# Per-column softmax scaling on ScalarE, split GpSimd subtractions, one more scratch buffer, and a new order of the first loads

## The chip, the core and the metric

The kernel runs on one core of one Trainium2 chip. A core has TensorE (PE, matrix multiplication, with its weight loads shown apart as PEld), VectorE (DVE), ScalarE (ACT), GpSimd (POOL) and SyncE (SP, which here only issues transfers). Each engine takes its own instructions in order; they wait for each other through semaphores. The metric is the device time of one execution in microseconds (us).

## The reference

One decoder layer on x of 512 tokens by 1024 channels. One projection of x gives the inputs of three mixers that run side by side, and the gates:

```python
u = jnp.einsum('bsd,de->bse', x, w_in) + b_in
y_a = _pool_mixer(a_x, pool_w, pool_b, pool_scale) * silu(a_z)      # trailing means, windows 2, 4, 8, 16
y_b = _dsa_mixer(b_q, b_k, b_v, i_q, i_k, i_w) * silu(b_z)          # attention over the top keys of an indexer
y_c = _nsa_mixer(c_q, ..., c_g, ...) * silu(c_z)                    # compressed, selected and window attention
g = sigmoid(g_merge)
m = g[0] * (y_a @ w_pa) + g[1] * (y_b @ w_pb) + g[2] * (y_c @ w_pc)
out = layernorm(ALPHA * x + m @ w_o) * ln_g + ln_b
```

In the third mixer each of the three softmaxes is multiplied by a sigmoid gate of its own for each token and head:

```python
o = gb[..., 0:1] * o_c + gb[..., 1:2] * o_s + gb[..., 2:3] * o_w
```

## The kernel before

**Tiling.** Tokens lie in the free dimension for projections: one tile is 128 output channels by 512 tokens, made by `dense` (line 142) from 8 slices of 128 input channels. Values are kept as a rounded high part and a low remainder, and `mm3` (line 67) multiplies with three matmuls (high by high, high by low, low by high), so one dense tile is 24 matmuls of 512 columns. There are 55 such tiles (a few narrower), then merges with the three output projections (`branch_d`, line 608), and at the end the product with `wo` (line 876) and the layer norm.

**Weights.** `load_w` (line 87) brings a tile into one of two staging buffers (`wst`), ScalarE copies it to the high part (line 93), and the remainder is subtracted (line 95): on VectorE in the first and last stage, on GpSimd while `POOL[0]` is set. In that middle stage the transfers are issued from GpSimd's queue as well (line 92). The first two weight tiles and x go another way: `load_early` (line 118) and `load_x` (line 112), issued by SyncE in the order written at line 129, in which letters are halves of the two weight tiles and digits are the eight slices of x.

**Order.** TensorE's order is written by hand: generators yield after each small group of matmuls, and `Stream.step` (line 699) mixes the projections ("fill" work, `F`) with attention. The other engines' orders are laid down by a planner when the program is built: by priority (`tc.high_priority()` puts work first) and by when its model sees operands and buffers free. A tile of a tag gets one of that tag's buffers; when all are in use, its writer waits for a release. Tag `b` holds scratch of up to 4 KB a partition: the `z` of `silu2` (line 403), `x0` and the chain of `xs` in `pool_x` (line 559), `za` of `pool_z`, gates `tg`, and small tiles. PSUM has three buffers for projections (`dps`), four for scores (`qps`), and one for the attention sums.

**Softmax.** `Unit.front` (line 423) makes the scores of a 128-token block for 2 or 4 heads at a time: matmuls (line 443), mask and row minimum on VectorE (445), exponential with row sum on ScalarE (450), reciprocal of the sums on VectorE (454), times the gate on VectorE (458; units of the second mixer have no gate and use a constant, 456), scaled probabilities in half precision on ScalarE (462), and their remainder on VectorE (464), which is the last reader of the score PSUM buffer. Units "c" with a gate come first, then units "b". There are 26 groups with a gate, 64 head columns in all. `topk_round` (303) puts searches for the top keys between them on VectorE.

**Before the first load lands**, TensorE multiplies a tile of zeros 8 times (lines 99 to 103). At the end (lines 890 to 901), for two of the four token tiles, 7 of 8 slices of the product with `wo` are multiplied, then the last slice, which needs the last merged part.

Of the kernel before, what the change touches and what calls it, by code (L numbers as in the profile page):

```python
# [7 lines left out]
F32 = mybir.dt.float32  # L8
F32R = mybir.dt.float32r
BF = mybir.dt.bfloat16  # L10
F16 = mybir.dt.float16
AF = mybir.ActivationFunctionType
# [7 lines left out]
KT = D // 128  # L20
# [10 lines left out]
EARLY = (0, I_KK)  # L31
# [3 lines left out]
def trunk(ctx, tc, a, out, dbg=None):  # L35
    nc = tc.nc
# [4 lines left out]
    sp = ctx.enter_context(tc.tile_pool(name="sp", bufs=2))  # L41
# [1 line left out]
    pq = ctx.enter_context(tc.tile_pool(name="pq", bufs=4, space=PSUM))  # L43
    pv = ctx.enter_context(tc.tile_pool(name="pv", bufs=1, space=PSUM))

    BUFS = {"x": 8, "wst": 2, "wh": 3, "wl": 3, "s": 2, "p": 2, "pt": 2, "t": 16, "ks": 2, "b": 6}

    def big(tag, name, dt=F32, shape=(128, 2, 512)):
        return bp.tile(list(shape), dt, tag=tag, name=name, bufs=BUFS[tag])

    def sm(name, n=8, bufs=4):
        return sp.tile([128, n], F32, tag=name, name=name, bufs=bufs)

    def dps(name):
        return pd.tile([128, 512], F32, tag="pd", name=name)

    def qps(name):
        return pq.tile([128, 512], F32, tag="pq", name=name)

    def f(ap):  # L60
        return ap.bitcast(F32)

    def split(h, l, src):
        nc.scalar.activation(h, src, AF.Copy)
        nc.vector.tensor_sub(l, src, f(h))  # L65

    def mm3(ps, wh, wl, rh, rl, start, stop):
        nc.tensor.matmul(ps, wh, rh, start=start, stop=False)  # L68
        nc.tensor.matmul(ps, wh, rl, start=False, stop=False)  # L69
        nc.tensor.matmul(ps, wl, rh, start=False, stop=stop)  # L70
# [14 lines left out]
    POOL = [False]  # L85

    def load_w(src, n, tag="w"):
        st = big("wst", f"{tag}_st", F32, (128, 1024))[:, :n]
        h = big("wh", f"{tag}_h", F32R, (128, 1024))
        l = big("wl", f"{tag}_l", F32R, (128, 1024))  # L90
        with tc.high_priority():
            (nc.gpsimd if POOL[0] else nc.sync).dma_start(st, src)  # L92
            nc.scalar.activation(h[:, :n], st, AF.Copy)  # L93
            eng = nc.gpsimd if POOL[0] else nc.vector
            eng.tensor_sub(l[:, :n], st, f(h[:, :n]))  # L95
        return h, l


    idle = big("b", "idle", BF, (128, 512))
    nc.vector.memset(idle, 0.0)  # L100
    ps = qps("idle")
    for _ in range(8):
        nc.tensor.matmul(ps, idle[:, :128], idle, start=True, stop=True)


# [6 lines left out]
    def load_x(k):  # L112
        st = xst[k // 4][:, k % 4]
        dma = nc.sync.dma_start(st, a["xT"][:, k, :])
        split(xh[k // 2][:, k % 2, :], xl[k // 2][:, k % 2, :], st)
        return dma

    def load_early(i, c, n):
        if i not in early:
            early[i] = [big(t, f"w{i}{c}", d, (128, 1024)) for t, c, d in (  # L120
                ("s", "s", F32), ("t", "h", F32R), ("t", "l", F32R))]
        s = slice(c * 1024 // n, (c + 1) * 1024 // n)
        st, h, l = early[i]
        nc.sync.dma_start(st[:, s], a["wt"][i][:, s])
        split(h[:, s], l[:, s], st[:, s])

    bias = const("bias")
    with tc.high_priority():
        for k in "a01b23c4d567":
            if k in "abcd":  # L130
                load_early(EARLY["abcd".index(k) % 2], "abcd".index(k) // 2, 2)
            else:
                dma = load_x(int(k))
    ctx.enter_context(tc.issue_after(dma.ins))

    def X(part, k, s0=0, s1=S):
# [214 lines left out]
    def compress_mid(nm):  # L351
        w1h, w1l, bh, bl = CP[nm]
        ps = dps("cp" + nm)[:64, :62]
        for l in range(16):
            mm3(ps, w1h[:, l, :], w1l[:, l, :], bh[:, :, l], bl[:, :, l], l == 0, l == 15)
            if l % 4 == 3:
                yield
        th = sp.tile([64, 62], F32, name="th", bufs=1)
        nc.scalar.activation(th, ps, AF.Tanh, scale=0.5)
        z = big("b", "hz", F32, (64, 2, 4, 32))  # L360
        nc.vector.memset(z, 0.0)
        for g in range(2):
            c = slice(31 * g, 31 * g + 31)
            nc.vector.scalar_tensor_tensor(z[:, g, :, :31], th[:, None, c].to_broadcast([64, 4, 31]), 1.0,
                                           ps[:, None, c].to_broadcast([64, 4, 31]), op0=OP.add, op1=OP.mult)
        zh = big("b", "hth", F32R, (64, 2, 4, 32))
        zl = big("b", "htl", F32R, (64, 2, 4, 32))
        split(zh, zl, z)
        CP[nm] = zh, zl
# [13 lines left out]

    def compress_v():
        HH, HL, w2h, w2l = CP["v"] + W2[1]
        v32 = sp.tile([128, 2, 64], F32, name="vc32", bufs=1)
        ps = dps("vc")[:, :128].rearrange("p (g d) -> p g d", g=2)
        for g in range(2):
            mm3(ps[:, g], HH[:, g].rearrange("p r n -> p (r n)"), HL[:, g].rearrange("p r n -> p (r n)"),
                w2h, w2l, True, True)  # L390
        nc.vector.tensor_scalar(v32, ps, vscale, 0.5, op0=OP.mult, op1=OP.mult)
        for p in range(3):
            v1 = sp.tile([128, 2, 64], BF, name="vc1", bufs=2)
            nc.vector.tensor_copy(v1, v32)
            if p < 2:
                nc.vector.tensor_sub(v32, v32, v1)
            for h in range(4):
                r = slice(32 * h, 32 * h + 32)
                nc.gpsimd.tensor_copy(VC[p][r, :, h], v1[r])
        yield  # L400
# [11 lines left out]
    class Unit:  # L412
# [10 lines left out]
        def front(self, u):  # L423
            nm, j, Q, K, gate = self.nm, self.j, self.Q, self.K, self.gate
            n, nk = (j + 1) * 128, j + 1
            nsub = self.nsub
            nh = 4 // nsub
# [4 lines left out]
            c, w = (0, slice(0, n)) if not cmp else (32, slice(0, n + 32)) if j < NT - 1 else (0, slice(32, n + 32))  # L432
# [20 lines left out]
            r = sm("r", 4)  # L453
            nc.vector.reciprocal(r[:, :nh], den[:, :nh])
            if gate is None:
                nc.vector.tensor_scalar(r[:, :nh], r[:, :nh], PSC, None, op0=OP.mult)
            else:
                nc.vector.tensor_mul(r[:, :nh], r[:, :nh], gate[:, u * nh:(u + 1) * nh])
            p = big("p", "p" + nm, F16, (128, 2, nh, n))
            for b in range(2):  # L460
                for i in range(b * hb, b * hb + hb):
# [269 lines left out]
    W2 = [compress_w2("k", 128), compress_w2("v", 64)]  # L731
    st = Stream([(dsa_keys,)])
    st2 = Stream([(f_kk, 0)])
    for n in (2, 1, 1, 1, 1, 1, 2):
        for _ in range(n):
            st.step()
        for _ in range(n):
            st2.step()
# [149 lines left out]
        nc.vector.bn_stats(bst[t][:, c0 // 256 * 6:c0 // 256 * 6 + 6], Zt[t][:, c0:c1])  # L888

    bst = [sm("bst", 24) for _ in range(NT)]  # L890
    pss = [dps("wo"), dps("wo")]
    for k0, k1 in ((0, KT - 1), (KT - 1, KT)):
        for t in range(2):
            wo_mm(pss[t], 0, t, k0, k1)
    for t in range(NT):
        if t > 1:
            pss.append(dps("wo"))
            wo_mm(pss[t], 0, t, 0, KT)
        add_x(t, pss[t], 0, 512)
        for c in (0, 256):  # L900
            stats(t, c, c + 256)
    for t in range(NT):
# [17 lines left out]
        if not last:  # L920
            c = cs.pop()
# [81 lines left out]
```

## Time and profile before

| what | value |
|---|---|
| median of 3 runs | 529.67 us (529.11 to 530.96) |
| the profiled execution's own time | 529.6 us, of which the span is 527.8 us |
| moved by transfers | 66.72 MB, 126 GB/s on average |
| DMA queues, share of 16 engines | 28.9% (hardware queue), 16.4% (software queue) |

The busy time of an engine is the time in which at least one of its instructions runs, and the span runs from the first to the last instruction. A row of the groups names the line, the engine, the operation and its operands, how many there were, their busy time, and the idle time of the engine just before them with what ended it. In a timeline row the first number is the start, the second the duration, and the bracket tells the idle time before it.

### The profile page before, as it was taken

What the parts mean: (1) busy time and instruction counts of PE and PEld (TensorE: products, weight loads), DVE (VectorE), ACT (ScalarE), POOL (GpSimd) and SP (SyncE); (2) the same over time, 40 slices, a digit from 0 to 9 for tenths busy, and PEclk for the clock granted to TensorE, in tenths of its full rate; (3) what the DMA queues carried; (4) which work ended last, traced back from release to release, by engine and by line L of the source; (5) the groups of instructions that cost most, each with busy time, mean ns of one, the idle gap of its engine ahead of it and who ended that gap; (6) DMA issues with size and microseconds to landing.
All of it is one profiled execution on the core that took longest, in us unless ns stands there. A gap on an engine that the chain in (4) does not pass through costs nothing. (4 is left out here: it accounts for less than half of the span.)

```text
span 527.8 us, 7784 instructions
## 1 busy us (share of the span) xinstructions
PE 508.5 (96%) x2718; PEld 420.1 (80%) x2718; DVE 378.7 (72%) x912; ACT 281.5 (53%) x585; POOL 219.8 (42%) x205
## 2 busy tenths in 40 slices
PE   8999999988999999899999999999999999999993
PEld 5889878876888888688888788888788888887883
DVE  5773799789868798999787897956654345444276
ACT  6684475756566666673755647566663344432000
POOL 1424443463556467344544344427662112115042
PEclk9999999999999999899999999999999999999997
DMA  8622332168845342556534434453584445462012
GB/s 289 261 80 81 110 130 61 46 117 137 170 111 162 86 126 52 119 133 170 142 101 122 139 110 105 134 120 106 145 169 121 140 139 180 159 215 105 1 70 90
DMA packets 82135, 66.72 MB, mean 126 GB/s; under 512 B 67184, under 2 KB 68656, under 8 KB 82096
## 3 DMA queue, kind: packets, MB, share of 16 engines
q1 hardware_dynamic: 74912, 40.54, 28.9%
q0 software_dynamic: 7184, 25.69, 16.4%
q8 instruction: 21, 0.34, 0.3%
q14 instruction: 18, 0.15, 0.1%
HBM read 47.87 MB, written 2.10 MB: 95 GB/s over the span
## 5 line engine op out<-in xcount | busy, mean ns | idle before, releaser
L68 PE MATMUL d<-xh,w_h 128*128 128x512 f32 (+1 forms) x424 | 167.1, 394 | 2.6 <-ACT z L153 2.4
L69 PE MATMUL d<-xl,w_h 128*128 128x512 f32 (+1 forms) x424 | 165.2, 390 | 0.0
L70 PE MATMUL d<-xh,w_l 128*128 128x512 f32 (+1 forms) x424 | 165.1, 389 | 0.0
L95 POOL TENSOR_TENSOR w_l<-w_st,w_h 128x1024 fp32r<-128x1024 f32 x41 | 98.0, 2393 | 111.0 <-ACT w_h L93 109.9
L68 PEld LDWEIGHTS d<-xh,w_h 128*128 128x128 f32 x424 | 80.0, 189 | 18.5 <-ACT z L153 2.9
L70 PEld LDWEIGHTS d<-xh,w_l 128*128 128x128 f32 x424 | 79.9, 188 | 16.8
L69 PEld LDWEIGHTS d<-xl,w_h 128*128 128x128 f32 x424 | 79.9, 189 | 13.9
L93 ACT ACTIVATE w_h<-w_st 128x1024 fp32r<-128x1024 f32 x53 | 56.1, 1058 | 35.1 <-DMA w_st<-in_wt_dram 27.8
L450 ACT ACTIVATE qkc<-qkc,nb 128x512 f32<-128x512 f32 (+3 forms) x64 | 32.0, 500 | 51.2 <-DVE nb L445 32.5
L95 POOL TENSOR_TENSOR wp_l<-wp_st,wp_h 128x512 fp32r<-128x512 f32 x16 | 20.8, 1297 | 49.4 <-ACT wp_h L93 49.4
L464 DVE SCALAR_TENSOR_TENSOR pc<-qkc,r,pc 128x512 f16<-128x512 f32 (+3 forms) x64 | 32.7, 545 | 10.8 <-ACT pc L462 10.6
L643 POOL TENSOR_TENSOR m<-m,tg 128x512 f32<-128x512 f32 x12 | 16.5, 1377 | 52.8 <-DVE tg L617 52.6
L462 ACT ACTIVATE pc<-qkc,r 128x512 f16<-128x512 f32 (+3 forms) x64 | 29.8, 526 | 14.6 <-issue 7.1
L445 DVE CUSTOM_DVE_ANT_0 qkc<-qkc,cmask 128x512 f32<-128x512 f32 (+3 forms) x64 | 31.2, 495 | 2.7 <-PE qkc L443 2.3
L92 POOL DMA_DIRECT2D w_st<-in_wt_dram x41 | 23.3, 569 | 9.9 <-POOL w_l L95 5.3
L70 PE MATMUL wo<-woh,ml 128*128 128x512 f32 (+1 forms) x72 | 26.4, 367 | 0.4 <-DVE ml L65 0.4
L69 PE MATMUL wo<-wol,mh 128*128 128x512 f32 (+1 forms) x72 | 26.3, 366 | 0.0
L68 PE MATMUL wo<-woh,mh 128*128 128x512 f32 (+1 forms) x72 | 26.3, 366 | 0.0
L306 DVE MATCH_REPLACE8 acc<-m,acc 128x256 f32<-128x256 f32 (+2 forms) x48 | 26.0, 543 | 0.0
L95 DVE TENSOR_TENSOR w_l<-w_st,w_h 128x1024 fp32r<-128x1024 f32 x12 | 15.8, 1323 | 13.4 <-ACT w_h L93 13.4
L450 ACT ACTIVATE qkb<-qkb,nb 128x128 f32<-128x128 f32 (+3 forms) x32 | 16.0, 500 | 17.6 <-DVE nb L445 17.3
L305 DVE MAX8 m<-acc 128x8 f32<-128x256 f32 (+2 forms) x48 | 25.3, 549 | 0.0
(249 smaller groups left out, 1029.2 us busy)
## 6 DMA issues: line engine op xcount, KB each, us to landing
w_st<-in_wt_dram POOLq DMA_DIRECT2D x41, 512.0 KB, 3.8
w_st<-in_wt_dram SPq DMA_DIRECT2D x12, 512.0 KB, 3.8
wp_st<-in_wp_dram POOLq DMA_DIRECT2D x16, 256.0 KB, 3.0
wo_st<-in_wo_dram SPq DMA_DIRECT2D x8, 512.0 KB, 3.6
xst<-in_xT_dram SPq DMA_DIRECT2D x8, 256.0 KB, 4.7
wp_st<-in_wp_dram SPq DMA_DIRECT2D x8, 256.0 KB, 2.7
z<-in_x_dram SPq DMA_DIRECT2D x4, 512.0 KB, 5.0
wvst<-in_wve_dram SPq DMA_DIRECT2D x4, 320.0 KB, 7.1
```

Of the source, the lines that this page charges most:

```text
L68: nc.tensor.matmul(ps, wh, rh, start=start, stop=False)
L69: nc.tensor.matmul(ps, wh, rl, start=False, stop=False)
L70: nc.tensor.matmul(ps, wl, rh, start=False, stop=stop)
L92: (nc.gpsimd if POOL[0] else nc.sync).dma_start(st, src)
L93: nc.scalar.activation(h[:, :n], st, AF.Copy)
L95: eng.tensor_sub(l[:, :n], st, f(h[:, :n]))
L305: nc.vector.max(m8, negm[j])
L306: nc.vector.match_replace(negm[j], m8, negm[j], MARK)
L445: nc.vector.tensor_tensor_reduce(sc[i], sc[i], self.mask, -0.125, 3e38, OP.add, OP.min, nb[:, i:i + 1])
L450: nc.scalar.activation(sc[i], sc[i], AF.Exp, scale=-1.0, bias=nb[:, i:i + 1], accum_out=den[:, i:i + 1])
L462: nc.scalar.activation(p[:, 0, i], sc[i], AF.Copy, scale=r[:, i:i + 1])
L464: self.last = nc.vector.scalar_tensor_tensor(p[:, 1, i], sc[i], r[:, i:i + 1], p[:, 0, i], op0=OP.mult, op1=OP.subtract)
```

## The change

Seven edits:

- line 46: tag `b` has seven buffers instead of six. The tiles `th`, `vc32` and `vc1`, which had buffers of their own, now take `b` buffers too (lines 358, 386, 393).
- line 94: with GpSimd, the remainder of a weight tile is subtracted in pieces of 512 columns: two for a 1024-column tile, one for a 512-column tile.
- line 102: nine multiplications of zeros instead of eight.
- line 129: the two first weight tiles are loaded, copied and subtracted in quarters, one ahead of each slice of x, alternating between the two tiles.
- line 458: the product of reciprocal and gate is made by ScalarE, one instruction for each head column, instead of one VectorE instruction for a group.
- line 734: the first two dense tiles alternate slice by slice from the first slice on.
- line 891: three of the four token tiles take 7 of 8 slices of `wo` first, and the third PSUM buffer is taken for it.

```diff
-    BUFS = {"x": 8, "wst": 2, "wh": 3, "wl": 3, "s": 2, "p": 2, "pt": 2, "t": 16, "ks": 2, "b": 6}
+    BUFS = {"x": 8, "wst": 2, "wh": 3, "wl": 3, "s": 2, "p": 2, "pt": 2, "t": 16, "ks": 2, "b": 7}
...
-            eng = nc.gpsimd if POOL[0] else nc.vector
-            eng.tensor_sub(l[:, :n], st, f(h[:, :n]))
+            if POOL[0]:
+                for c in range(0, n, 512):
+                    nc.gpsimd.tensor_sub(l[:, c:c + 512], st[:, c:c + 512], f(h[:, c:c + 512]))
+            else:
+                nc.vector.tensor_sub(l[:, :n], st, f(h[:, :n]))
...
-    for _ in range(8):
+    for _ in range(9):
         nc.tensor.matmul(ps, idle[:, :128], idle, start=True, stop=True)
...
-        for k in "a01b23c4d567":
-            if k in "abcd":
-                load_early(EARLY["abcd".index(k) % 2], "abcd".index(k) // 2, 2)
-            else:
-                dma = load_x(int(k))
+        for k in range(KT):
+            load_early(EARLY[k % 2], k // 2, 4)
+            dma = load_x(k)
...
-        th = sp.tile([64, 62], F32, name="th", bufs=1)
+        th = big("b", "th", F32, (64, 62))
...
-        v32 = sp.tile([128, 2, 64], F32, name="vc32", bufs=1)
+        v32 = big("b", "vc32", F32, (128, 2, 64))
...
-            v1 = sp.tile([128, 2, 64], BF, name="vc1", bufs=2)
+            v1 = big("b", "vc1", BF, (128, 2, 64))
...
-                nc.vector.tensor_mul(r[:, :nh], r[:, :nh], gate[:, u * nh:(u + 1) * nh])
+                for i in range(nh):
+                    nc.scalar.activation(r[:, i:i + 1], gate[:, u * nh + i:u * nh + i + 1], AF.Copy,
+                                         scale=r[:, i:i + 1])
...
-    for n in (2, 1, 1, 1, 1, 1, 2):
+    for n in (1, 1, 1, 1, 1, 1, 1, 2):
...
-    pss = [dps("wo"), dps("wo")]
+    pss = [dps("wo") for _ in range(3)]
     for k0, k1 in ((0, KT - 1), (KT - 1, KT)):
-        for t in range(2):
+        for t in range(3):
             wo_mm(pss[t], 0, t, k0, k1)
     for t in range(NT):
-        if t > 1:
+        if t > 2:
```

## The prediction, made before the changed kernel was run

> **What bounds the kernel now.** First the page: span, busy time, and the clock row of the slices.
>
> ```profile
> span 527.8 us, 7784 instructions
> PE 508.5 (96%) x2718; PEld 420.1 (80%) x2718; DVE 378.7 (72%) x912; ACT 281.5 (53%) x585; POOL 219.8 (42%) x205
> PEclk9999999999999999899999999999999999999997
> ```
>
> TensorE (PE) is busy all but 527.8 - 508.5 = 19.3 us. So no more than 19.3 us can come out of idle time, and other gains need matmuls that run slower than they could. The clock row has one low slice ahead of the end, the 19th, at about 205 to 218 us. The view of waits, PE alone, names the idle time:
>
> ```profile
> PE qkc L443 <- DVE pc L464: 3.5, 3, 1.8
> PE d L68 <- ACT z L153: 2.4, 1, 2.4
> PE pp L68 <- DVE m L617: 1.2, 1, 1.2
> PE idle L103 <- DVE idle L100: 1.2, 1, 1.2
> PE d L68 <- ACT xh L64: 1.0, 1, 1.0
> PE cpk L69 <- DVE bkl L65: 0.5, 1, 0.5
> PE wo L70 <- DVE ml L65: 0.4, 1, 0.4
> ```
>
> The columns are total, times, longest. They sum to 10.2 us; the other 9.1 us lie behind the last matmul (layer norm and output) and no edit changes that chain. So eight waits (beside the 1.2 us ahead of the first zero product), and slow matmuls after them, are what can be won. The timeline shows each. The start:
>
> ```profile
> 1.18 3.59 PE L103 MATMUL idle<-idle 128*128 128x512 bf16 x8 [1.18 <-DVE idle L100]
> 5.73 0.79 PE L68 MATMUL d<-xh,w0h 128*128 128x512 f32 x1 [0.95 <-ACT xh L64]
> 8.75 0.63 PE L68 MATMUL d<-xh,w3h 128*128 128x512 f32 x1
> 9.18 0.59 PE L69 MATMUL d<-xl,w3h 128*128 128x512 f32 x1
> 10.09 0.40 PE L69 MATMUL d<-xl,w3h 128*128 128x512 f32 x1
> 10.32 0.40 PE L70 MATMUL d<-xh,w3l 128*128 128x512 f32 x1
> ```
>
> The zeros end at 4.77, and the first real matmul starts at 5.73, when ScalarE has copied the first slice of x. Starts are 0.43 us apart at 9 us and 0.23 us apart at 10 us: up to about 9.5 us TensorE works at about half its later rate, though the clock row shows none of it. Next, the longest of the three waits for scores (PE idle 1.79 us at 129.31):
>
> ```profile
> 124.96 2.39 POOL L95 TENSOR_TENSOR w_l<-w_st,w_h 128x1024 fp32r<-128x1024 f32 x1 [0.62 <-ACT w_h L93]
> 125.20 2.16 DVE L458 TENSOR_TENSOR r<-r,gs 128x2 f32<-128x2 f32 x1
> 129.31 0.65 PE L443 MATMUL qkc<-ks,cq 128*128 128x416 f32 x2 [1.79 <-DVE pc L464]
> ```
>
> VectorE's product of two columns takes 2.16 us and ends at 127.36, with GpSimd's subtraction (127.35). ScalarE's copy (L462) needs that product, VectorE's remainder (L464) the copy, and TensorE's next scores the PSUM buffer that L464 reads last. The group row says how often:
>
> ```profile
> L458 DVE TENSOR_TENSOR r<-r,gs 128x2 f32<-128x2 f32 (+1 forms) x26 | 13.3, 510 | 0.4
> 204.06 0.16 DVE L458 TENSOR_TENSOR r<-r,gs 128x2 f32<-128x2 f32 x1
> ```
>
> Undisturbed it takes 0.16 us; 26 times that is 4.2, and the sum is 13.3, so 9.1 us are spent blocked. The wait of 1.53 us at 113.47 is another case:
>
> ```profile
> 110.33 0.66 ACT L450 ACTIVATE qkc<-qkc,nb 128x512 f32<-128x512 f32 x1 [4.22 <-DVE nb L445]
> 111.01 1.05 ACT L93 ACTIVATE w_h<-w_st 128x1024 fp32r<-128x1024 f32 x1
> 111.95 0.68 ACT L462 ACTIVATE pc<-qkc,r 128x512 f16<-128x512 f32 x1
> 113.47 0.73 PE L443 MATMUL qkc<-kw,cq 128*128 128x512 f32 x2 [1.53 <-DVE pc L464]
> ```
>
> Here ScalarE stood idle for 4.22 us, and then a weight copy was planned ahead of the probabilities. Last, the wait of 2.44 us:
>
> ```profile
> 206.61 0.68 ACT L407 ACTIVATE zc<-d,bhalf 128x512 f32<-128x512 f32 x1
> 210.87 1.27 POOL L569 TENSOR_TENSOR xs<-xs 128x504 f32<-128x504 f32 x1
> 211.43 0.73 DVE L458 TENSOR_TENSOR r<-r,gs 128x2 f32<-128x2 f32 x1
> 212.25 1.27 ACT L462 ACTIVATE pc<-qkc,r 128x512 f16<-128x512 f32 x2 [1.05 <-issue]
> 213.40 0.69 ACT L153 ACTIVATE z<-d,bias 128x512 f32<-128x512 f32 x1
> 214.14 0.60 PE L68 MATMUL d<-xh,w_h 128*128 128x512 f32 x1 [2.44 <-ACT z L153]
> 214.54 0.63 PE L69 MATMUL d<-xl,w_h 128*128 128x512 f32 x1
> 214.97 0.63 PE L70 MATMUL d<-xh,w_l 128*128 128x512 f32 x1
> 200.00:220.00 20.00, 17.56 (x86) 13.78 (x85) 17.11 (x44) 11.26 (x25) 11.27 (x14) 0.91 0.50 109
> ```
>
> A dense tile's PSUM is read twice by ScalarE: L407 at 206.61, and L153 (into a `b` scratch) only at 213.40, though both have high priority. In between the `xs` chain of `pool_x`, which lives in `b` too, runs to its fourth step; L153 comes right after that step's source is free (212.14). I read this as L153 waiting for a `b` buffer, on top of ScalarE's queue waiting for the blocked L458. After it matmuls start 0.43 us apart, and the granted clock of those 20 us is 0.91 (third number from the right): 9% of 20 us is 1.8 us below full clock.
>
> **The change part by part.** The sum is made against the profiled execution's own 529.6 us (1.8 us lie around its span); the median of the runs is 529.67, so it carries over.
>
> Start (quarters, ninth zero product, order of slices). Ahead of the end of x's first slice came 512 KB (half a weight tile, 256 KB of x), now 384 KB. At the rate of the stretch in which it lands,
>
> ```profile
> 5.00:10.00 5.00, 4.27 (x10) 3.06 (x11) 3.53 (x7) 3.91 (x7) 0.00 (x0) 1.00 0.98 363
> ```
>
> (last number, GB/s; the two before it are the DMA share and the granted clock) 128 KB are 0.36 us, and the whole gap of 0.95 is the most that can go; I take 0.5, so the first real matmul starts near 5.2. Nine zero products at 3.59/8 = 0.45 end at 5.2 as well: the gap of 0.95 closes. One matmul more is done by 9.5 us, which is worth 0.3. The larger term is the slow rate. It ended about 3.8 us after the gap at the start, and 3.4 us after the one at 214 us. If it is the gap that starts the count anew, the count now runs from 1.18 and full rate comes 3 to 4 us earlier: (0.43 - 0.23)/0.43 of 3.4 us = 1.6 us. Bounds: a ninth product that delays the first slice, +0.2; nothing; all nine slow matmuls at full rate, -1.8. I take -1.6 - 0.3 = -1.9. Four more copies and subtractions cost ScalarE about 4 x 0.2 us (0.63 for 512 columns, 1.06 for 1024, so 0.2 of each is fixed); x's last slice is then some 0.8 us later, and TensorE reaches it about 2 us later than it is there, so this stays hidden.
>
> [...]
>
> Reciprocal times gate. VectorE loses 26 instructions, 13.3 us. ScalarE gains 64. Its nearest rows:
>
> ```profile
> L914 ACT ACTIVATE rs<-ve 128x1 f32<-128x1 f32 x4 | 0.8, 203 | 37.4 <-DVE ve L913 37.4
> 196.56 1.14 ACT L462 ACTIVATE pc<-qkc,r 128x128 f16<-128x128 f32 x4
> ```
>
> so 0.20 each (one column) to 0.29 (1.14/4); I take 0.20 as the nearer: 13.0 us, at most 18.6, on an engine that is 53% busy. In a group of two heads the chain gets 2 x 0.20 - 0.16 = 0.24 us longer, in one of four 0.64; 20 and 6 groups give 8.6 us, about the 9.1 us of blocking that go. On average nothing is won; but TensorE waits only at the worst cases, and those are the blocked ones. The 129.31 wait goes whole, -1.8 (its price without cover: none, the blocked product was its cause; if halves of 1.3 us still block the remainder's neighbours, half of it stays). The waits at 113.47 and 120.98 (3.5 - 1.8 = 1.7 together) depend on the planner's order: the columns could use ScalarE's idle 4.22 us; bounds 0 and -1.7, I take the middle, -0.9.
>
> [...]
>
> GpSimd in halves:
>
> ```profile
> L95 POOL TENSOR_TENSOR w_l<-w_st,w_h 128x1024 fp32r<-128x1024 f32 x41 | 98.0, 2393 | 111.0 <-ACT w_h L93 109.9
> L95 POOL TENSOR_TENSOR wp_l<-wp_st,wp_h 128x512 fp32r<-128x512 f32 x16 | 20.8, 1297 | 49.4 <-ACT wp_h L93 49.4
> ```
>
> 2 x 1297 - 2393 = 201 ns more, 41 times: 8.2 us of GpSimd time, before 111 us of idle time in front of these very instructions. The next transfer from its queue comes 0.2 us later; no PE wait is for weights. For VectorE a block now lasts at most 1.3 us. I cost it at nothing: bounds +0.5 (the smallest listed wait of that kind), and -0.5.
>
> Seventh `b` buffer. L153 can follow L407 at about 207.3, six microseconds before TensorE needs the buffer. The 2.4 us go, and the slow matmuls: 214.14 to 217.5 is 3.4 us at 0.43 instead of 0.23, 1.6 us. Together -4.0, bounds 0 (something else held L153) and -4.2. `th`, `vc32`, `vc1` take buffers while the compression runs (70 to 110 us), when no `xs` is alive: nothing, bound +0.5.
>
> Third `wo` tile: 21 matmuls, 4.8 us, lie ahead of the part that waits 0.4: -0.4. The other waits (1.2 for L617 at 292.48, 0.5 for bkl) I leave.
>
> New waits: 64 more instructions in ScalarE's queue can make a PSUM reader late once; I put +1.0, between nothing and the 1.8 that the worst score wait costs. Sum: -1.9 - 1.8 - 0.9 - 4.0 - 0.4 + 1.0 = -8.0, so **521.6**.
>
> **The rivals.** [...]
>
> *L153 stays late*, or the next tile takes its place: 521.6 + 4.0 = 525.6. For it: the buffer is my reading; ScalarE's in-order queue also stood behind L458. Against: L407 had run.
>
> *The softmax stage is bound by VectorE*, so an earlier TensorE only waits later: start and end alone remain, 529.6 - 2.3 = 527.3. For it:
>
> ```profile
> 220.00:240.00 20.00, 20.00 (x90) 16.63 (x89) 19.58 (x52) 15.16 (x32) 9.89 (x9) 1.00 0.43 106
> ```
>
> VectorE is 98% busy there; against it, TensorE waits for nothing in the same stretch, and VectorE gets 13.3 us back.
>
> *The plan is merely reshuffled*: new order, other waits of the same total, 529.6. This is also the case in which the edits don't do what they say.
>
> *Slower*: columns at the head of ScalarE's queue wait for VectorE's reciprocal, as L462 did at 212 us, and hold L153 and L407 behind them; each such case costs 4.0 with the slow matmuls. The other gains are 9.0, so from the third case on (9.0/4.0 = 2.3) the kernel is slower: with three, 529.6 - 9.0 + 12.0 = 532.6. For it: four columns add 0.64 us to that head. Against: the same chain without the product is free of GpSimd's block.
>
> **How the numbers follow.** Forecast 0.43, start slow 0.17, L153 late 0.14, VectorE-bound 0.07, reshuffled 0.09, slower 0.10. A measurement tells 0.3%, 1.6 us, so "the same" is 528.1 to 531.3: faster 0.81, same 0.09, slower 0.10. The range leaves out the slower case, half of the reshuffled one, and times below 518 (the sum with every bound at its best is -2.1 - 1.8 - 1.7 - 4.2 - 0.4 - 0.5 = -10.7, 518.9, and part of the 1.2 at L617 may go too): 518 to 529.
>
> **What would show it.** Right: the first real matmul near 5.2 and starts 0.23 apart by 6 us; no L458 on VectorE, and 64 one-column instructions of about 0.2 us on ScalarE; L153 within a microsecond of L407 in every `silu2`; no low clock slice at 205 to 218; PE busy with under 14 us of idle time. Wrong: PE waits for ACT or for DVE pc above 3 us in sum, or a new low slice of the clock. A PE wait for w_l would make the halves the culprit.

## The result, and the profile after

The changed kernel takes **522.78 us** (median of 4 runs, 520.31 to 523.73), the kernel before, run beside it, 529.75 us (529.11 to 530.96): a ratio of 0.9863, 95% interval 0.9829 to 0.9898. That is 7.0 us, and the forecast of 521.6 was 1.2 us too low. The page of the changed kernel, same lines as those shown of before:

```profile
span 522.0 us, 7880 instructions
PE 509.4 (98%) x2719; PEld 420.4 (81%) x2719; DVE 358.8 (69%) x890; ACT 295.0 (57%) x653; POOL 230.9 (44%) x246
PEclk9999989999999999999999999999999999999998
L96 POOL TENSOR_TENSOR w_l<-w_st,w_h 128x512 fp32r<-128x512 f32 x82 | 108.5, 1341 | 110.9 <-ACT w_h L93 106.0
```

TensorE's idle time fell from 19.3 us to 522.0 - 509.4 = 12.6, but its busy time rose by 0.9 us for the same matmuls and one product of zeros more (0.45 us): some of them now run slower. The clock row says where. The low slice of before, the 17th of 40, at 211 to 224 us, is gone, and a new one stands in the 6th, at 65 to 78 us. VectorE lost 19.9 us of busy time, ScalarE gained 13.5. The waits of the changed kernel above 0.2 us, PE alone (total, times, longest):

```profile
PE idle L106 <- DVE idle L103: 1.2, 1, 1.2
PE cpk L69 <- DVE bkl L65: 1.0, 1, 1.0
PE wo L70 <- DVE ml L65: 1.0, 1, 1.0
PE d L70 <- DVE w_l L98: 0.4, 1, 0.4
PE pool L68 <- ACT ph L64: 0.4, 1, 0.4
```

The waits for `pc` (3.5), for `z` (2.4), for L617 (1.2) and for the first x (1.0) are all gone. Two small ones have grown: for `bkl` from 0.5 to 1.0 and for `ml` from 0.4 to 1.0. The windows of the changed kernel (busy time and count of PE, PEld, DVE, ACT, POOL, then granted clock, DMA share, GB/s) show what the slices show, with numbers:

```profile
72.00:76.00 4.00, 4.00 (x49) 3.87 (x50) 3.92 (x7) 1.85 (x4) 3.08 (x3) 0.74 0.34 122
76.00:80.00 4.00, 4.00 (x13) 3.23 (x13) 3.92 (x6) 2.69 (x6) 0.00 (x0) 0.50 0.36 131
105.00:130.00 25.00, 25.00 (x113) 20.75 (x112) 21.14 (x59) 20.01 (x45) 17.68 (x25) 1.00 0.67 158
200.00:220.00 20.00, 19.40 (x99) 14.89 (x98) 17.24 (x44) 14.60 (x36) 12.07 (x17) 1.00 0.40 96
```

From 105 to 130 us TensorE never stops now, and at 200 to 220 us it makes 99 matmuls where it made 86. But from 74 to 80 us it runs at half clock. The kernel before in the same windows:

```profile
76.00:80.00 4.00, 4.00 (x19) 2.98 (x18) 4.00 (x7) 3.56 (x8) 0.00 (x0) 1.00 0.35 120
105.00:130.00 25.00, 21.49 (x93) 17.01 (x92) 22.82 (x54) 15.16 (x30) 13.98 (x17) 1.00 0.74 127
216.00:220.00 4.00, 4.00 (x16) 3.23 (x15) 4.00 (x12) 0.78 (x2) 0.55 (x1) 0.77 0.76 171
```

To sort the gain by place, the same matmul is looked up in two traces, and its start in the one is taken from its start in the other. How that lead changes over a stretch is what the stretch gained or lost. For the profiled runs, after less before, in us, at the times of the kernel before:

```
stretch of before            lead at its end   change   what lies in it
5.73 to 68.91   start to ve        -0.05       +0.79    first matmul at 4.89 (-0.84), lead of 2.14 at 9.85, given back by 28.9
68.91 to 111.55 compression        +2.82       +2.87    bkl wait 1.0, half clock at 74 to 80
111.55 to 129.31 first softmaxes   -1.39       -4.21    three pc waits gone
129.31 to 217.10 softmaxes, z      -5.16       -3.76    z wait gone, low clock gone
217.10 to 289.98                   -4.57       +0.58    two waits for ph, 0.4 and 0.2
289.98 to 292.48 L617              -5.74       -1.16    wait for m gone
292.48 to 518.67 merges, wo        -5.07       +0.67    ml wait 1.0 instead of 0.4
the end of the span                -5.86       -0.79
```

So the middle of the kernel gives more than the whole gain, the compression takes nearly three back, and the start brings nothing. In the last row, the chain from the last matmul to the last transfer's issue takes 4.46 us in both kernels (518.99 to 523.45, and 513.92 to 518.38); the 0.8 lies in how the last output lands, and I have no cause for it.

### The profile page after: what moved, and what is told of

Its sections match the earlier page's. It is cut to its first block, busy times and chain, and to the rows that moved or that the text cites. A ratio compares the mean times of both kernels' runs of the same rounds, so it can differ in the third digit from the quotient of the medians.

```text
span 522.0 us, 7880 instructions
## 1 busy us (share of the span) xinstructions
PE 509.4 (98%) x2719; PEld 420.4 (81%) x2719; DVE 358.8 (69%) x890; ACT 295.0 (57%) x653; POOL 230.9 (44%) x246
## 4 chain that ended last, share of the span: by engine, by line
PE 54%; DVE 5%; DMA 2%; ACT 1%; issue 0%; DVEq 0%; ACTq 0%
PE d L68 9%; PE d L69 9%; PE d L70 9%; PE pp L68 4%; PE pp L69 4%; PE pp L70 4%; PE acc L484 3%; PE wo L70 3%; PE wo L68 3%; PE wo L69 2%; PE qkb L444 2%; DMA wo_st<-in_wo_dram 2%; PE qkc L444 1%; DVE pc L467 1%; DVE wol L65 1%; DVE acc L307 1%
## 5 line engine op out<-in xcount | busy, mean ns | idle before, releaser
L96 POOL TENSOR_TENSOR w_l<-w_st,w_h 128x512 fp32r<-128x512 f32 x82 | 108.5, 1341 | 110.9 <-ACT w_h L93 106.0
L68 PE MATMUL pp<-yh,wp_h 128*128 128x512 f32 x64 | 25.1, 392 | 0.0
```

Source lines behind the costliest of these rows:

```text
L96: nc.gpsimd.tensor_sub(l[:, c:c + 512], st[:, c:c + 512], f(h[:, c:c + 512]))
```

## The experiments

Two accounts of the middle were to be told apart: that of the prediction (the product moved to ScalarE frees the score buffers, the seventh buffer frees `z`, the halves are worth nothing), and a rival, that the shorter GpSimd instructions do it. First each part was taken out of the changed kernel, then each was put alone into the kernel before. The kernels were run in three groups, each with the kernel before beside them: 529.74 us in the first group (15 runs), 530.46 in the second (25), 530.15 in the third (22). Ratios are to these.

**The start undone.** Loads, zeros and order of slices as before:

```diff
-    for _ in range(9):
+    for _ in range(8):
...
-        for k in range(KT):
-            load_early(EARLY[k % 2], k // 2, 4)
-            dma = load_x(k)
+        for k in "a01b23c4d567":
...
-    for n in (1, 1, 1, 1, 1, 1, 1, 2):
+    for n in (2, 1, 1, 1, 1, 1, 2):
```

> The changed kernel with the start of before (halves, eight zero products, old order of the first slices). Theory A, from the two traces set side by side: the new start gains 2.1 us by 10 us and has lost it all by 29 us, because its transfers come in more slowly; then this kernel is at the time of the changed kernel, within 0.7 us, and its matmuls after 29 us run as in the changed kernel. Theory B, the prediction's: the start is worth 1.9 us; then this kernel is about 1.9 us slower than the changed one (ratio to before near 0.990).

Measured: 522.64 us (522.04 to 523.2), 0.9856 [0.9819, 0.9893]: level with the change. This trace with eight zeros was also at full rate by 6.57 us. The traces hold a record of the granted clock, which begins with the first full clock (ahead of that the views show 1.00, though matmuls start 0.43 us apart). In the eight traces with nine zeros full clock begins at 4.92 to 7.09 us. With eight zeros it begins at 9.07 to 10.35 in four, at 4.99 in this one, and at 4.47 in one that is at half clock again from 7.89 to 11.30. So in these traces full clock mostly came earlier where the gap was closed, but a start with the gap can have it too. The record begins anywhere from 4.47 to 10.35 us, and every later change in it lies a multiple of 3.41 us behind its beginning: in the kernel before it begins at 9.60, and the changes lie 60, 61 and 150 times 3.41 us behind that; in the changed kernel it begins at 5.68, and they lie 20, 22 and 150 times behind. Counted back from 9.60 in the same steps, the gap of 0.95 us of the kernel before lies in the stretch from 2.77 to 6.19, and full clock begins behind the next one.

What the rate gains is lost again before the first product behind the two dense tiles. ScalarE's timeline in the changed kernel, and the DMA view of its first 16 us:

```profile
11.96 0.63 ACT L64 ACTIVATE xh<-xst 128x512 fp32r<-128x512 f32 x1
12.50 0.40 ACT L64 ACTIVATE w3h<-w3s 128x256 fp32r<-128x256 f32 x1
15.01 0.63 ACT L64 ACTIVATE xh<-xst 128x512 fp32r<-128x512 f32 x1 [2.11 <-DMA xst<-in_xT_dram]
```

```profile
DMA packets 2869, 4.51 MB, mean 282 GB/s; under 512 B 440, under 2 KB 1464, under 8 KB 2869
```

and of the kernel before:

```profile
11.05 1.96 ACT L64 ACTIVATE xh<-xst 128x512 fp32r<-128x512 f32 x3
```

```profile
DMA packets 2477, 4.96 MB, mean 310 GB/s; under 512 B 396, under 2 KB 396, under 8 KB 2477
```

Before, the last three slices of x are copied from 11.05 to 13.01. Now the last is copied at 15.01, after a wait of 2.11 us for its transfer: with 1464 instead of 396 packets under 2 KB, 4.51 MB land in the time of 4.96. The six traces with the new start have 3.97 to 4.61 MB in their first 16 us, the other eight 4.65 to 5.17; that the smaller packets are the reason wasn't tried by itself. TensorE then stalls at 16.42 and 18.59. Over the traces, the first `ve` product starts at 36.66 to 38.53 us (mean 37.6) in six with the new start and at 36.94 to 39.04 (38.0) in six with the old one: 0.4 us, inside the scatter.

**The product back on VectorE**, the rest of the change kept:

```diff
-                for i in range(nh):
-                    nc.scalar.activation(r[:, i:i + 1], gate[:, u * nh + i:u * nh + i + 1], AF.Copy,
-                                         scale=r[:, i:i + 1])
+                nc.vector.tensor_mul(r[:, :nh], r[:, :nh], gate[:, u * nh:(u + 1) * nh])
```

> The changed kernel with the product of reciprocal and gate back on VectorE, one instruction a group. Theory A: blocked products are what TensorE waited for at 113 to 129 us, and the change's lead of 4.2 us between the scores at 113 and 129 us comes from their removal; then waits for VectorE's remainder of pc come back with 1.5 us or more, and the kernel is 2 to 4 us slower than the changed one. Theory B: the halves on GpSimd alone end the long blocks (at most 1.3 us), or the new plan does; then it is within 1 us of the changed kernel and those waits stay away.

Measured: 521.98 us (521.19 to 522.8), 0.9844 [0.9806, 0.9881]. Nothing is lost, though small waits come back (0.9 us for `pc` in two, 0.5 for `z`). The group row of the product there:

```profile
L459 DVE TENSOR_TENSOR r<-r,gs 128x2 f32<-128x2 f32 (+1 forms) x26 | 8.9, 344 | 0.4
```

It takes 8.9 us instead of 13.3, with no edit of its own.

**Six buffers** in the changed kernel:

```diff
-    BUFS = {"x": 8, "wst": 2, "wh": 3, "wl": 3, "s": 2, "p": 2, "pt": 2, "t": 16, "ks": 2, "b": 7}
+    BUFS = {"x": 8, "wst": 2, "wh": 3, "wl": 3, "s": 2, "p": 2, "pt": 2, "t": 16, "ks": 2, "b": 6}
...
-        th = big("b", "th", F32, (64, 62))
+        th = sp.tile([64, 62], F32, name="th", bufs=1)
```

`vc32` and `vc1` go back in the same way.

> The changed kernel with six scratch buffers (and th, vc32, vc1 with buffers of their own). Theory A: a missing scratch buffer held the second read of the projection's PSUM at 214 us; then a wait of TensorE for ACT z of 2 us or more comes back near 205 to 215 us, mostly with a low clock after it, and the kernel is 2.5 to 4.5 us slower than the changed one. Theory B: the blocked product on VectorE held ScalarE's queue there; then the wait stays away and it is within 1 us of the changed kernel.

Measured: 527.04 us (524.97 to 529.86, 10 runs), 0.9942 [0.9915, 0.9969]: 4.3 us are lost, and the wait for `z` that was forecast is there, with half clock from 213.14 to 216.55 us behind it:

```profile
PE d L68 <- ACT z L154: 3.3, 1, 3.3
```

But its mechanism is another. Its ScalarE timeline has the two reads of the dense tile at

```profile
208.38 0.68 ACT L408 ACTIVATE zc<-d,bhalf 128x512 f32<-128x512 f32 x1
211.70 1.24 ACT L465 ACTIVATE pc<-qkc,r 128x512 f16<-128x512 f32 x2
212.84 0.68 ACT L154 ACTIVATE z<-d,bias 128x512 f32<-128x512 f32 x1
```

and with seven buffers, in the changed kernel,

```profile
205.03 0.68 ACT L408 ACTIVATE zc<-d,bhalf 128x512 f32<-128x512 f32 x1
208.34 1.24 ACT L465 ACTIVATE pc<-qkc,r 128x512 f16<-128x512 f32 x2
209.49 0.68 ACT L154 ACTIVATE z<-d,bias 128x512 f32<-128x512 f32 x1
```

The second read comes 4.46 us after the first in both; all three rows lie 3.35 us later. The delay begins at 137 us, where halves from 136.37 to 138.87 block two small products of VectorE (L521 and L524: 0.60 and 1.33 us instead of 0.16 and 0.29), and most of it comes at 140 us, in GpSimd's and VectorE's timeline of the kernel with six buffers:

```profile
140.59 2.54 POOL L96 TENSOR_TENSOR w_l<-w_st,w_h 128x512 fp32r<-128x512 f32 x2
140.80 2.49 DVE L527 TENSOR_TENSOR cp<-cs,cp 128x128 f16<-128x128 f32 x1
```

One small subtraction waits through both halves. With seven buffers the plan puts the halves at 141.99, behind it:

```profile
139.28 0.43 DVE L527 TENSOR_TENSOR cp<-cs,cp 128x128 f16<-128x128 f32 x1
141.99 2.99 POOL L96 TENSOR_TENSOR w_l<-w_st,w_h 128x512 fp32r<-128x512 f32 x2 [1.71 <-ACT w_h L93]
```

Why a buffer changes GpSimd's order there isn't settled.

**Whole subtractions** in the changed kernel:

```diff
-                for c in range(0, n, 512):
-                    nc.gpsimd.tensor_sub(l[:, c:c + 512], st[:, c:c + 512], f(h[:, c:c + 512]))
+                nc.gpsimd.tensor_sub(l[:, :n], st, f(h[:, :n]))
```

> The changed kernel with GpSimd's subtractions of 1024 columns in one piece. Theory A: worth nothing by themselves, as the prediction costed them; within 0.7 us of the changed kernel, with single VectorE instructions of two SBUF inputs blocked for 2 us again. Theory B: the halves carry part of the gain at 113 to 129 us or at 292 us; then it is 1 to 3 us slower, with waits for VectorE there.

Measured: 525.27 us (524.27 to 526.9), 0.9909 [0.988, 0.9939]. 2.5 us of the gain are lost, and the wait for `z` is back and larger than before, though the seventh buffer is there:

```profile
PE d L68 <- ACT z L151: 4.1, 1, 4.1
```

**The halves alone**, in the kernel before:

```diff
-            eng = nc.gpsimd if POOL[0] else nc.vector
-            eng.tensor_sub(l[:, :n], st, f(h[:, :n]))
+            if POOL[0]:
+                for c in range(0, n, 512):
+                    nc.gpsimd.tensor_sub(l[:, c:c + 512], st[:, c:c + 512], f(h[:, c:c + 512]))
+            else:
+                nc.vector.tensor_sub(l[:, :n], st, f(h[:, :n]))
```

> Before with only GpSimd's subtractions in halves. Theory A: shorter blocks take the waits for VectorE's pc at 113 to 129 us (3.5 us before) to under 1.5 us, while the wait for ACT z near 210 us stays at 2 us or more or grows, since a scratch buffer still lacks: 526 to 528.5 us. Theory B (any rearranged plan loses those waits): the product alone and the halves alone do the same at 113 to 129 us.

Measured: 524.52 us (522.58 to 527.88), 0.9899 [0.9871, 0.9927]: 5.9 us, most of the gain, from the edit that was costed at nothing, and the wait for `z`, which Theory A left at 2 us or more, falls too. Its waits:

```profile
PE cpk L69 <- DVE bkl L65: 0.7, 1, 0.7
PE d L68 <- ACT z L156: 0.7, 1, 0.7
PE qkc L446 <- DVE pc L467: 0.5, 1, 0.5
```

and its row of the product, which nobody moved:

```profile
L461 DVE TENSOR_TENSOR r<-r,gs 128x2 f32<-128x2 f32 (+1 forms) x26 | 7.4, 283 | 0.4
```

A new plan isn't what does it. Compared by what they write and read, in the order of their starts, only 9 of VectorE's 886 instructions and 4 of ScalarE's 585 stand at another place than in the kernel before (the product left out of the count). The weight copy that the prediction blamed for the wait at 113.47 us still stands ahead of the probabilities (at 110.52 us), and the wait there is 0.48 us instead of 1.53.

**Halves and seventh buffer** in the kernel before: that diff, and

```diff
-    BUFS = {"x": 8, "wst": 2, "wh": 3, "wl": 3, "s": 2, "p": 2, "pt": 2, "t": 16, "ks": 2, "b": 6}
+    BUFS = {"x": 8, "wst": 2, "wh": 3, "wl": 3, "s": 2, "p": 2, "pt": 2, "t": 16, "ks": 2, "b": 7}
```

with `th`, `vc32` and `vc1` in `b`.

> Before with only the seventh scratch buffer and GpSimd's subtractions in halves. Theory A (these two carry the change; the product on ScalarE, the new start and the third wo tile give nothing that remains): within 1 us of the changed kernel, 521.5 to 524 us, and in the trace neither the waits for VectorE's pc at 113 to 129 us above 1 us in sum, nor a wait for ACT z above 1 us. Theory B (the product on ScalarE is needed for the waits at 113 to 129 us once the rest is as before): those waits stand with 2 us or more, and the time is 525 to 527 us.

Measured: 523.91 us (522.71 to 526.01), 0.9894 [0.9861, 0.9927]: level with the halves alone.

**The product on ScalarE alone**, in the kernel before:

```diff
-                nc.vector.tensor_mul(r[:, :nh], r[:, :nh], gate[:, u * nh:(u + 1) * nh])
+                for i in range(nh):
+                    nc.scalar.activation(r[:, i:i + 1], gate[:, u * nh + i:u * nh + i + 1], AF.Copy,
+                                         scale=r[:, i:i + 1])
```

> Before with only the product of reciprocal and gate on ScalarE. Theory A: VectorE is still blocked for up to 2.4 us in its other instructions with two SBUF inputs; the waits for pc lose the one of 1.8 us whose product was blocked, the wait for ACT z stays: 526 to 529 us. Theory B, the prediction's price: 2.7 us gained at 113 to 129 us, so 527 us with the later wait unchanged, less if that one grows by the lead.

Measured: 526.77 us (524.0 to 529.04), 0.9939 [0.9915, 0.9963]. The `pc` waits are all gone. By the same comparison this edit does bring a new plan: 99 of VectorE's 886 other instructions and 31 of ScalarE's 585 stand at another place, so what the freed product gives and what the new order gives can't be told apart. Of TensorE's lead a part is waited away for `z`:

```profile
PE d L68 <- ACT z L153: 4.1, 1, 4.1
```

**The seventh buffer alone**, in the kernel before:

```diff
-    BUFS = {"x": 8, "wst": 2, "wh": 3, "wl": 3, "s": 2, "p": 2, "pt": 2, "t": 16, "ks": 2, "b": 6}
+    BUFS = {"x": 8, "wst": 2, "wh": 3, "wl": 3, "s": 2, "p": 2, "pt": 2, "t": 16, "ks": 2, "b": 7}
...
-        th = sp.tile([64, 62], F32, name="th", bufs=1)
+        th = big("b", "th", F32, (64, 62))
```

and `vc32` and `vc1` alike.

> Before with only the seventh scratch buffer (and th, vc32, vc1 taken from it). Theory P, the prediction's: the wait for ACT z of 2.4 us near 214 us goes with its slow matmuls, 4.0 us, so 525.7 us, and L153 follows L407 within a microsecond. Theory A, from the runs so far (halves without the seventh buffer leave 0.7 us of that wait, the product on ScalarE without it 4.1): ScalarE's in-order queue, which stands behind VectorE's blocked instructions, sets when z is read; then the buffer alone moves the wait by less than 1 us and the time is 528.5 to 531 us.

Measured: 529.34 us (527.14 to 534.78), 0.9999 [0.9967, 1.003]: nothing. Its two reads on ScalarE's timeline:

```profile
207.00 0.69 ACT L407 ACTIVATE zc<-d,bhalf 128x512 f32<-128x512 f32 x1
212.64 1.27 ACT L462 ACTIVATE pc<-qkc,r 128x512 f16<-128x512 f32 x2 [1.05 <-issue]
213.79 0.69 ACT L153 ACTIVATE z<-d,bias 128x512 f32<-128x512 f32 x1
```

6.79 us apart, as before (206.61 and 213.40). A free buffer doesn't move L153: of VectorE's and of ScalarE's order it changes one instruction each, at 76 to 88 us.

With the kernel before, all eight combinations of the three edits were run, counting those told of below. In one profiled run of each, by the same lookup of matmuls (change over the stretch in us; kernels differ in the start and in `wo` too, which lie elsewhere):

```
product on ScalarE, halves, seventh buffer     111.55 to 129.31   129.31 to 217.10
no,  no,  yes  (b7 alone)                           -0.19              -1.25
no,  yes, no   (halves alone)                       -3.43              -3.04
no,  yes, yes  (four kernels)                  -2.6 to -4.2       -2.9 to -3.5
yes, no,  no   (product alone)                      -4.21              +1.91
yes, no,  yes  (whole subtractions)                 -4.21              +1.85
yes, yes, no   (six buffers)                        -4.21              +0.98
yes, yes, yes  (the change)                         -4.21              -3.76
yes, yes, yes  (start undone; mixed and new wo)     -4.21          -3.74; -3.77
```

In the first stretch the product is worth 4.2 and the halves 3.4 of the same 4.2: they remove the same waits. In the second the product by itself loses 1.9, the halves win 3.0, and the seventh buffer matters only where both others are in. (The -1.25 of the first row is no wait: that trace waits 2.4 us for `z` like the kernel before, but has full clock at 216 to 220 us, where before has 0.77.)

**Quarters of 256 columns** in the changed kernel, to see whether shorter is better still:

```diff
-                for c in range(0, n, 512):
-                    nc.gpsimd.tensor_sub(l[:, c:c + 512], st[:, c:c + 512], f(h[:, c:c + 512]))
+                for c in range(0, n, 256):
+                    nc.gpsimd.tensor_sub(l[:, c:c + 256], st[:, c:c + 256], f(h[:, c:c + 256]))
```

> The changed kernel with GpSimd's subtractions in pieces of 256 columns instead of 512. Theory A: the length of a block is the lever; blocks of at most 0.75 us leave no waits for VectorE's pc and shorten those for ACT z, at some 0.3 us more of GpSimd for each tile: 521 to 523 us, VectorE's busy time 3 to 8 us below that of the changed kernel. Theory B: the halves merely gave another plan; then it lands anywhere from 521 to 527 us, with new waits.

Measured: 524.6 us (521.16 to 526.41), 0.988 [0.9841, 0.9918]: no better. VectorE is blocked less, and from 111.55 to 217.10 us its trace gains 7.8 us, as much as the change (8.0). But GpSimd is busy 245.5 us instead of 230.9, and behind that new waits come, so that 3.8 us are lost from 217.10 to 289.98 and 2.0 in the merges and `wo`:

```profile
PE pool L68 <- ACT ph L64: 2.0, 1, 2.0
PE acc L484 <- DMA ptb<-pb: 1.0, 1, 1.0
```

How long VectorE is blocked in all can be estimated from the traces: for each of its instructions that start from 60 to 300 us, its time less the shortest of the same line, operation and shape, summed. That gives 36.6 us before, 24.5 with the product alone, 20.1 with the halves alone, 17.9 in the change and 14.9 with quarters; the longest single excess is 2.25 us before, 1.06 in the change and 1.16 with quarters.

**The low clock at 72 to 80 us.** The 48 matmuls of the key compression, 62 columns wide, follow the `bkl` wait. In the changed kernel they are now mixed into a dense tile, so that TensorE has wide matmuls between them; and `wo` is cut into slices 0 to 5, 6 and 7 instead of 0 to 6 and 7, so that slice 6 is multiplied later:

```diff
+    def mid_zc():
+        a_, b_ = f_zc(0, 1), compress_mid("k")
+        for n, _ in enumerate(a_):
+            yield
+            if n % 2:
+                for _ in b_:
+                    yield
+                    break
...
-    F = Stream([(compress_in, I_KC, "k"), (vscales,), (compress_in, I_VC, "v"), (f_zc, 0, 0), (compress_mid, "k"),
-                (f_zc, 0, 1), (compress_k,), (compress_mid, "v"), (f_qc, 1, 0), (f_qc, 1, 1), (compress_v,),
+    F = Stream([(compress_in, I_KC, "k"), (vscales,), (compress_in, I_VC, "v"), (f_zc, 0, 0), (mid_zc,),
+                (compress_k,), (compress_mid, "v"), (f_qc, 1, 0), (f_qc, 1, 1), (compress_v,),
...
-    for k0, k1 in ((0, KT - 1), (KT - 1, KT)):
+    for k0, k1 in ((0, KT - 2), (KT - 2, KT - 1), (KT - 1, KT)):
```

> The changed kernel with two edits of order on TensorE: the small matmuls of the key compression (62 columns) are mixed with a dense tile, two slices of that tile ahead of each group, and the last product takes slices 0 to 5 of three token tiles, then slice 6, then slice 7. Theory A: the wait for bkl (1.0 us) goes, and with it the half clock that follows it in some runs at 72 to 80 us (3.3 us in the profiled run of the changed kernel); the wait of 1.0 us at the end was for slice 6 inside the first token tile and goes too: 517 to 520.5 us. Theory B: an earlier TensorE only waits at about 210 us for the second read of a projection's PSUM: 520 to 523 us with such a wait of 1 to 3 us.

Measured: 531.29 us (529.62 to 533.65), 1.0026 [1.0001, 1.005]. The mixture fails: by the waits,

```profile
PE kc L68 <- ACT hth L64: 3.9, 1, 3.9
PE cpk L68 <- DVE bk L337: 2.9, 1, 2.9
```

TensorE now waits 6.8 us in the compression, and the granted clock is 0.50 at 76 to 80 us and 0.55, 0.50 and 0.50 in the windows from 88 to 100. The stretch to 111.55 loses 14.1 us where the change loses 2.9. By these waits, the dense tile had been what covered the step behind the small matmuls. The `wo` part works: no wait for `ml` is left, and the stretch behind 292.48 gains 0.3 us (0.7 and 0.2 in the two kernels below) instead of losing 0.7.

**Halves, seventh buffer, ninth zero, new slices of `wo`**, with the old loads and the product on VectorE, in the kernel before:

```diff
-    for _ in range(8):
+    for _ in range(9):
...
-    pss = [dps("wo"), dps("wo")]
-    for k0, k1 in ((0, KT - 1), (KT - 1, KT)):
-        for t in range(2):
+    pss = [dps("wo") for _ in range(3)]
+    for k0, k1 in ((0, KT - 2), (KT - 2, KT - 1), (KT - 1, KT)):
+        for t in range(3):
```

> What the runs show to be worth something, without the rest: halves, seventh buffer, nine zero products with the old order of the first loads, three wo tiles with slices 0 to 5, then 6, then 7; the product of reciprocal and gate stays on VectorE. Theory A: nine zero products bring full rate by 6.6 us, and the loads in halves land x's last slice by 12.5 us, so the first values matmul is at 36.5 to 37.3 us (38.0 before, 38.0 in the changed kernel); no wait for ml at the end; 520 to 522.5 us, about 1 us ahead of the changed kernel. Theory B: the early lead is given back later, at the waits for bkl, pc or z: 522 to 524 us.

Measured: 522.85 us (520.29 to 523.14, 5 runs), 0.9843 [0.9815, 0.987]. The clock came as forecast: it is full from 6.62 us, and the first `ve` product starts at 37.05. Its profiled run has a span of 518.5 us and no low slice ahead of the end, but the median is level with the change: no version here is shown to beat it.

**The same with the second `zc` tile ahead of the key compression**, so that `bkl` is ready in time:

```diff
-    F = Stream([(compress_in, I_KC, "k"), (vscales,), (compress_in, I_VC, "v"), (f_zc, 0, 0), (compress_mid, "k"),
-                (f_zc, 0, 1), (compress_k,), (compress_mid, "v"), (f_qc, 1, 0), (f_qc, 1, 1), (compress_v,),
+    F = Stream([(compress_in, I_KC, "k"), (vscales,), (compress_in, I_VC, "v"), (f_zc, 0, 0), (f_zc, 0, 1), (compress_mid, "k"),
+                (f_qc, 1, 0), (compress_k,), (compress_mid, "v"), (f_qc, 1, 1), (compress_v,),
```

> The kernel called combo with one dense tile (f_zc 0 1) moved ahead of the key compression and another (f_qc 1 0) in its old place. Theory A: the low part of the compression's input (bkl) is then there 4 us before it is needed; the wait of 0.7 to 1.0 us goes, and with it the half clock that follows in some runs (2 to 3.3 us): 518.5 to 520.5 us. Theory B: attention begins one tile (5.5 us) later and VectorE has less time for its backlog, so that waits for pc or z come back: 521 to 524 us.

Measured: 528.24 us (525.56 to 530.21), 0.9955 [0.9931, 0.9979]. It is slower than either account said. The `bkl` wait is gone, another has come, and half clock behind it:

```profile
PE sc L505 <- POOL ks L385: 2.1, 2, 1.7
```

```profile
94.00:98.00 4.00, 4.00 (x30) 3.70 (x30) 2.69 (x10) 2.05 (x7) 0.00 (x0) 0.50 0.30 114
98.00:102.00 4.00, 4.00 (x12) 3.15 (x11) 1.94 (x6) 1.29 (x4) 0.00 (x0) 0.50 0.08 16
```

## Why the prediction was right in the time and wrong in its parts

That the time came within 1.2 us is luck: errors of several us cancelled. One reading was off from the start: the low slice of the clock is the 17th, at 211 to 224 us, not the 19th, and no term of its sum hangs on that. By the prediction's steps:

- **Start, -1.9: mis-sized, it measured about -0.4 (mean of the traces), and nothing by medians.** The size of the faster rate held: first matmul at 4.89 us, full rate from 5.97 (a count that a gap starts anew isn't what the clock's record shows: in the kernel before, its changes keep to the steps of 3.41 us across the wait of 2.44 us). The step that failed is "x's last slice is then some 0.8 us later ... so this stays hidden". It is copied at 15.01 instead of about 12.4 (13.2 to 15.5 in the six traces with the new start). In the changed kernel's trace ScalarE waits 2.11 us for that slice's transfer, so the four copies more aren't what delays it there. The sum without the 1.6 us of the faster rate, 521.6 + 1.6 = 523.2, came nearer than the forecast (0.4 us off against 1.2), though the rate wasn't what failed.
- **The waits at 113 to 129, -1.8 and -0.9: -4.2 was shown.** A blocked VectorE was the cause, as read: with its order all but kept, the halves remove 3.4 of the 4.2. Moving the product removes all three waits, but with a new order of two engines, so its own share isn't shown. The prediction took the middle for two of the waits; the whole was right. Beside the halves the move is worth nothing in the time.
- **The cost of the 64 columns was right:** 13.0 us of ScalarE forecast, 12.9 more shown with that edit alone (281.5 to 294.4). One takes 285 ns by its row, not 200, but two in a row take 0.48 us.
- **Halves, "I cost it at nothing": wrong, and the largest error.** Alone they give 5.9 us. Where it failed: the prediction asked who waits for GpSimd's weights (nobody) and left aside that its own account, a blocked VectorE, is cured from GpSimd's side as well. The bound of 0.5 was taken from a small wait of another kind; the waits behind L458 were the ones to take. Its "a block now lasts at most 1.3 us" held in the changed kernel (longest excess 1.06 us), but not in the one with six buffers (2.49, below).
- **Seventh buffer, -4.0: the reading was wrong.** L153 didn't wait for a `b` buffer: alone the buffer gives nothing, and the distance from L407 to L153 (6.8 us before) is 4.5 in the change, not under 1. L153 stands right behind the copies of `pc` in every trace, in ScalarE's order, and these wait for VectorE's chain. Halves alone shorten the distance to 5.15 and bring the wait from 2.4 to 0.7 us. That the buffer is worth 4.3 us inside the change is true of the size and not of the mechanism.
- **Third `wo` tile, -0.4: it came out at +0.6.** The step "21 matmuls lie ahead of the part that waits" overlooked that the wait is for slice 6, inside the first tile, ahead of any filler. The changed kernel's timeline:

```profile
473.27 0.92 DVE L65 TENSOR_TENSOR ml<-m,mh 128x512 fp32r<-128x512 f32 x1
474.25 0.50 PE L70 MATMUL wo<-woh,ml 128*128 128x512 f32 x1 [0.97 <-DVE ml L65]
```

  TensorE comes 5.7 us earlier than before, the slice only 5.1. Cutting at slice 6 removes the wait in the three kernels that tried it.
- **New waits, +1.0: more, and elsewhere.** It was meant for ScalarE's queue. The 2.9 us of the compression come from the half clock behind the `bkl` wait, which the prediction had at 0.5 us and left ("I leave"). Its own sign of being wrong, "a new low slice of the clock", is there, while PE waits neither for ACT nor for `pc` by more than 0.4 us.
- **L617, left at 1.2 us:** gone in every kernel that has the halves or the product (-1.16 in each).

Of the rivals, "VectorE-bound" describes the product alone: its lead of 4.3 us at 129 us is partly waited away for `z`, since the read of `z` came earlier by only 2.6 (210.85 instead of 213.40). The slower case didn't occur. What stays open: why six buffers change GpSimd's order at 137 to 140 us, and how much of the moved product's gain is due to its new order.

## What to carry to other kernels

When one engine is blocked by another's long instruction, price both cures: moving the victim and cutting the blocker. Here they removed the same waits (4.2 us and 3.4 of the same 4.2), so their gains didn't add, and the cut was the cheaper edit. Before a late read is put down to a missing buffer, look at what stands ahead of it in its engine's own order, and test the buffer alone; and price a small wait beside many narrow matmuls by the clock that may follow, not by its length (here 1.0 us of waiting, 2.9 us lost).

## What the hardware showed beside this

- **A block outlasted the instruction that started it.** In the kernel with six buffers, a VectorE subtraction that takes 0.43 us elsewhere took 2.49 us, from 140.80 to 143.29, beside two GpSimd halves (140.59 to 143.13). In the kernel before, the product of 0.16 us that took 2.16 ended at 127.36, with the one GpSimd instruction beside it (124.96 to 127.35); here the cut left no gap between the pieces, and the subtraction lasted through both.
- **About one microsecond of waiting was followed by half clock.** After the 1.01 us ahead of the 48 narrow matmuls, the windows show 0.74 and 0.50, and the stretch loses 2.9 us. It seems to come in some runs only: the four of the change took 523.73 and 523.6 us at a mean clock of 0.989, and 520.31 and 521.96 at 0.996. With the product back on VectorE the same wait was 0.9 us and the clock stayed at 1.00.
- **Half clock followed the stretches of 3.41 us in which few columns were multiplied.** The changes of the clock lie whole multiples of 3.41 us behind the beginning of the record; counted from there, each of the 14 traces can be cut into such stretches, and the output columns of the matmuls that start in one added up. Of 2047 stretches at full clock (up to 513 us), half clock followed all 13 with fewer than 3,100 columns, one of the three with 3,138 to 3,186, and none of the 2,031 with 3,324 or more. The narrow matmuls start about 0.06 us apart with 62 columns, some 1,000 columns per us, the wide ones 0.23 apart with 512, some 2,200. In the changed kernel the wait and the narrow matmuls share the stretch from 70.53 to 73.94, with 2,430 columns:

```profile
70.53:73.94 3.41, 2.40 (x36) 2.05 (x34) 3.38 (x6) 1.63 (x3) 1.69 (x2) 1.00 0.76 273
73.94:77.35 3.41, 3.41 (x23) 3.12 (x22) 3.36 (x5) 3.04 (x5) 1.39 (x2) 0.50 0.28 98
```

  With the product back on VectorE the stretch from 71.14 to 74.55 has 4,152. The waits of 2.4 us for `z` part in the same way: 1,536 columns in the kernel before, from 210.98 to 214.39, and half clock behind them; 3,584 with the seventh buffer alone, from 212.69 to 216.10, and full clock. So a wait of 2.4 us was followed by half clock in one trace and by full clock in the other, where it falls otherwise on the stretches.
